# Two-layer network on one core: the S5 output products in 64-row tiles, sums of squares on TensorE, nine low parts on GpSimd

## The chip, the cores and the metric

The kernel runs on one core of one Trainium2 chip. The metric is the device time of one execution in microseconds; it is given as the median of several runs, and one further execution was profiled.

## What is computed

The reference is a chain of two small networks over 512 positions and 1024 features: a convolution and pooling mixer, a gated linear recurrence, a normalisation, then an S5 state-space mixer, a gated unit, two MLPs, and windowed attention. What matters here is the S5 mixer, and the two normalisations ahead of it:

```python
x1 = rmsnorm(h, final_norm)            # end of the first network
hn = rmsnorm_2(x1, norm_mix[0])        # both need sums of squares over the features
# S5: 64 groups of 16 features, 64 complex states each
x_t = a * x_(t-1) + B u_t              # a, B complex, per group
y_t = Re(C x_t) + d * u_t              # = c_re . x_re - c_im . x_im
y   = gelu(y) @ w_glu ...
```

## The kernel before

Features lie on the partitions and time along the free axis. Every large matrix product is computed in three passes (`mm3`, lines 308 to 310): a weight chunk is loaded (`raw`), ScalarE copies its high part (`hi`), and VectorE or GpSimd subtracts to get the low part (`lo`). `prep` sends `lo` to GpSimd (POOL) for the chunk numbers in the set `on_pool`, else to VectorE (DVE). Chunks 107 to 109 are the last three of `w_out_odd`, 110 to 113 the small projections `w_proj`, 114 and 115 the first two of `w_glu`. There are two `raw` buffers, so the load of a chunk waits for the low part of the chunk two before it.

The work is laid out by a scheduler, and where it says `with self.after()` an instruction is pinned behind the TensorE instruction recorded before it. Each engine runs its queue in order.

**The way into S5.** The last product of the recurrence, `w_out_odd`, ends each of its eight output tiles m in `odd_out`: DVE adds the residual (`h`), ScalarE (ACT) makes a time-reversed copy (`xc`), POOL issues two DMAs that bring it back as the S5 input U (`du<-xc`, then `U<-du`), and two squares per tile are made by ACT (`xr`) and added up by DVE (`acc`), plain and scaled with the norm's weight. At the start of S5, TensorE turns the two accumulators into column sums (`columns`, line 368), and a chain of small DVE operations makes the factors by which U is scaled, six of the eight tiles on POOL and two on DVE.

**The S5 loop** runs over eight feature tiles ft. `states(ft)`: 16 TensorE matmuls (line 1251) make the inputs of the states in a PSUM bank; DVE turns them by a rotation (`a`, `b`), adds, runs two scans, turns them back (`c`, `b`), and combines real and imaginary parts of each half of the partitions in four operations of 64 partitions into the tile `e` (line 1273 sets its first column to zero). `leave(ft)`: for each of 8 groups, two matmuls with the matrix M of the chunk's inner part (line 1291) and two with the output matrix O over `e` (line 1293), 128 rows each, 64 columns of weights for either half f of the output; ACT then applies gelu and the result goes out and back by DMA. `states(ft + 1)` stands ahead of `leave(ft)` on TensorE. Between them stand blocks of the small projections (six `mm3` matmuls each, `fillers`), later pieces of the `w_glu` product (`part`). A float32 matmul shows as two rows in the trace.

**The tables** for S5 are computed in the first stage, interleaved with other work. `stored` writes the output matrices to DRAM (`tO`, line 1072), four DMAs of 64 partitions for each half q.

Of the kernel before, what the change touches and what calls it, by code (L numbers as in the profile page):

```python
# [11 lines left out]
AF = mybir.ActivationFunctionType  # L12
ALU = mybir.AluOpType
# [155 lines left out]
class Kern:  # L169
# [5 lines left out]
    SQX, EPOS = (0, 2, 5), (4, 4)  # L175
    TAPP = ()
    BOOST = 400
    on_pool = frozenset(n for n in range(107) if n > 57 or n % 2 or n < 6)

    def __init__(self, ctx, tc, I, O, vat, cat):  # L180
        self.tc, self.nc, self.I, self.O = tc, tc.nc, I, O
# [226 lines left out]
    def consts(self):  # L408
        nc = self.nc
        self.vecs = self.p_const.tile([128, self.I["vecs"].shape[1]], F32, name="vecs")  # L410
        nc.sync.dma_start(out=self.vecs, in_=self.I["vecs"])
        ct = self.p_const.tile([128, self.I["consts"].shape[1]], F32, name="ctile")
        nc.scalar.dma_start(out=ct, in_=self.I["consts"])
        C = lambda n: ct[:, self.cat[n][0]:self.cat[n][0] + self.cat[n][1]]
        self.ident, self.fix, self.eye16, self.chunk, self.not0 = (C(n) for n in ("ident", "fix", "eye16", "chunk", "not0"))
        self.half, self.own = C("half"), C("own")
        self.halfpi = self.p_const.tile([128, 1], F32, name="halfpi")
        nc.gpsimd.memset(self.halfpi, 1.5707963267948966)
        self.ones = self.p_const.tile([128, 128], F32, name="ones")
# [8 lines left out]
        self.tab, self.U, self.acc12 = [], [], []  # L428
        self.ft, self.behind, self.ticks = None, [], 0


# [301 lines left out]
    def odd(self, h):  # L733
        nc = self.nc
        xg = [self.split(h[k], self.X(), self.V("g_odd", k)) for k in range(8)]
        acc = self.square_sum(h)
# [4 lines left out]
        for n in range(-self.LAG, 12):  # L741
# [23 lines left out]
            x, i, gt = (t[:, n % G] for t in grp)  # L765
# [10 lines left out]
        for ms in self.ODD_MS:  # L776
            os = {m: self.bank(("mm", "mm", "mm", "sp", "sp", "yp", "yp", "mm")[m]) for m in ms}
            for q in range(2):
                for m in ms:
                    w = self.get_w()  # L780
                    for k in range(6):
                        self.mm3(os[m], w, k, ysp[6 * q + k], q + k == 0, q == 1 and k == 5)
                    if q == 1:
                        out[m] = self.odd_out(m, os[m], h[m])
        return out

    def lru(self, x, i, gt):
# [25 lines left out]
    def odd_out(self, m, o, h):  # L813

        n = self.H("h3")
        v = lambda a: a.rearrange("p (c s) -> p s c", s=8)
        self.add(n.rearrange("p (s c) -> p s c", s=8), v(o), v(h))
        if len(self.tab):


            r = self.L("xc", 2 + self.LAG)
            self.act(r.rearrange("p (s c) -> p s c", s=8), n.rearrange("p (s c) -> p s c", s=8)[:, ::-1], AF.Copy)
            du = self.dram.tile([128, T], F32, name=f"du{m}")
            self.nc.gpsimd.dma_start(out=du.rearrange("(s h) (g c) -> h g s c", s=8, g=8).rearrange("h g s c -> (h g) s c"),
                                     in_=r.rearrange("p (s c) -> p s c", s=8))
            U = self.p_xg.tile([128, 8, 64], F32, tag="xg", name="U")
            self.nc.gpsimd.dma_start(out=U.rearrange("p g c -> p (g c)"), in_=du)
            self.U.append(U)

            for k, g in enumerate((1.0, self.V("g_fin1", m))):  # L830
                q = self.L(*(self.sq if m else ("acc", 2)))
                self.act(q, n, AF.Square, scale=g)
                if m == 0:
                    self.acc12.append(q)
                else:
                    self.add(self.acc12[k], self.acc12[k], q)
        return n


# [19 lines left out]
    def odd_vectors(self):  # L859
# [16 lines left out]
        self.ts(q, lam, -1.0, ALU.mult, 0.0, ALU.max)  # L876
        self.stt(q, p, 2.0, q, ALU.mult, ALU.add)
        C = lambda nm, w: self.p_const.tile([128, w], F32, name=nm)
        self.sp4 = C("sp4", 12)
        self.ts(self.sp4, q, 4.0, ALU.mult)  # L880

# [95 lines left out]
    def tables(self, small):  # L977
# [16 lines left out]
        for ft in range(8):  # L994
# [14 lines left out]
            for q in range(2):  # L1009
# [58 lines left out]

                def stored(q=q, orr=orr, oi=oi, tO=tO):
                    for k, w in enumerate((orr, oi)):  # L1070
                        for g2 in range(2):
                            nc.sync.dma_start(out=tO[64 * k:64 * k + 64, 512 * q:512 * q + 512].rearrange("n (a g m) -> n g a m", a=2, g=2)[:, g2],
                                              in_=w[64 * g2:64 * g2 + 64].rearrange("p a j h -> p a (j h)"))

                late(stored)
                if q == 1:
# [77 lines left out]
    def s5(self, h, fill, glu):  # L1154
# [40 lines left out]
        def behind(f, *a, **k):  # L1195
            with self.after():
                f(*a, **k)
# [3 lines left out]
                behind(*next(blocks))  # L1201

        fillers(self.FILL[0])
        st = self.bank("st")
        for k in range(2):
            behind(self.columns, self.acc12[k], st, 4 * k)
        fillers(self.FILL[1])
        s = self.p_s.tile([128, 24], F32, tag="st", name="st_s")
        v, t = s[:, 0:8], s[:, 8:12]
# [30 lines left out]
        def states(ft):  # L1240
# [20 lines left out]
            self.mul(b[:, 1], sp[:, 0], N)  # L1261
            self.add(a[:, 0], a[:, 0], b[:, 0])
            self.sub(a[:, 1], a[:, 1], b[:, 1])
            for r in range(2):
                z = a[:, r].rearrange("p a c -> p (a c)")
                nc.vector.tensor_tensor_scan(out=z, data0=dec.rearrange("p a c -> p (a c)"), data1=z, initial=0.0, op0=ALU.mult, op1=ALU.add)


            e, c = f4(), f4()
            self.tt(c, a, c2, ALU.mult)  # L1270
            self.mul(b[:, 0], a[:, 1], N, nc.gpsimd if ft in self.B0P else None)
            self.mul(b[:, 1], a[:, 0], N, nc.gpsimd if ft in self.B1P else None)
            nc.vector.memset(e[:, :, :, 0:1], 0.0)
            for r, op in ((1, ALU.add), (0, ALU.subtract)):
                for q in range(2):
                    rows = slice(64 * q, 64 * q + 64)
                    self.tt(e[64 * r:64 * r + 64, q, :, 1:64], c[rows, r, :, 0:63], b[rows, r, :, 0:63], op)
            live[ft] = O, M, u, e

        def leave(ft):  # L1280
            O, M, u, e = live.pop(ft)
# [14 lines left out]
            nc.scalar.dma_start(out=dy, in_=y.rearrange("p g c -> p (g c)"))  # L1296
# [533 lines left out]
```

## Time and profile before

| | us |
|---|---|
| median of 3 runs | 1884.67 |
| lowest, highest | 1882.24, 1885.48 |
| the profiled execution's own time | 1886.16 |
| its span, first to last instruction | 1884.3 |
| TensorE busy in it | 1764.2 (94%) |
| VectorE, ScalarE, GpSimd busy | 1167.2, 762.0, 456.6 |

The profile has one line for each group of instructions, a list of who waited for whom, and a timeline. "PE" is TensorE, "PEld" its weight loads, SPq the DMA queue that loads the weights. An idle time in square brackets names what ended it. A line can be that of a helper, so instructions are told apart by the tiles that they write and read.

### The profile page before, as it was taken

Reading aid. Unit: us, or ns where it says so; the run is one execution under the profiler, and the core shown is the slowest. Engines: PE = TensorE matmul, PEld = TensorE weight load, DVE = VectorE, ACT = ScalarE, POOL = GpSimd, SP = SyncE. Lnnn points to the kernel's source line nnn. Section 1 sums busy time; section 2 is a strip of 40 time slices with the busy share of each in tenths; the row PEclk is TensorE's granted clock in tenths of the full one; section 3 lists DMA queues with packets and bytes.
Section 4 is the critical chain, followed back from the end, with each engine's and each line's share of the span. In section 5 each row is a group of like instructions: output and inputs, shape, how many; then the busy total and the mean of one; then the engine's idle time right before and its main releaser. Section 6 shows DMA issues by size and latency. Waiting matters only on the chain.

```text
span 1884.3 us, 24650 instructions
## 1 busy us (share of the span) xinstructions
PE 1764.2 (94%) x9298; PEld 1439.7 (76%) x9298; DVE 1167.2 (62%) x1885; ACT 762.0 (40%) x1330; POOL 456.6 (24%) x422
## 2 busy tenths in 40 slices
PE   7797999999887897899999999998999999999997
PEld 5685778877765776687888888887778888888886
DVE  9989777555888859655432344578686642244456
ACT  4334444443554462234432332335665432233234
POOL 5464667333666643100000000032000000000002
PEclk8898999999988898899999999999999999999998
DMA  4598443331222488523232222333111233322322
GB/s 167 136 225 213 128 129 123 119 104 65 76 75 76 136 244 291 169 92 112 93 100 91 100 100 91 101 106 110 41 55 45 101 101 91 100 101 91 100 94 91
DMA packets 128871, 215.93 MB, mean 115 GB/s; under 512 B 40048, under 2 KB 79728, under 8 KB 128752
## 3 DMA queue, kind: packets, MB, share of 16 engines
q1 hardware_dynamic: 108144, 189.27, 32.5%
q10 hardware_dynamic: 17968, 16.43, 2.6%
q0 software_dynamic: 2640, 8.65, 1.4%
q8 instruction: 73, 1.20, 0.3%
q14 instruction: 46, 0.38, 0.1%
HBM read 187.44 MB, written 26.21 MB: 113 GB/s over the span
## 4 chain that ended last, share of the span: by engine, by line
PE 68%; DVE 14%; issue 5%; POOL 4%; ACT 4%; DMA 3%; SPq 1%; ACTq 0%; DVEq 0%; POOLq 0%
PE mm L308 19%; PE mm L310 19%; PE mm L309 19%; POOL lo L252 2%; DVE lo L252 1%; DVE e L808 1%; ACT hi L249 1%; PE pv L1609 1%; SPq L1175 1%; PE sc L309 1%; PE sc L308 1%; PE sc L310 1%; DVE pl L264 1%; DVE srm L267 1%; DVE h L264 1%
## 5 line engine op out<-in xcount | busy, mean ns | idle before, releaser
L249 ACT ACTIVATE hi<-raw 128x1024 fp32r<-128x1024 f32 (+1 forms) x280 | 292.4, 1046 | 672.8 <-PE mm L309 552.4
L252 DVE TENSOR_TENSOR lo<-raw,hi 128x1024 fp32r<-128x1024 f32 (+1 forms) x211 | 262.1, 1243 | 422.1 <-ACT hi L249 417.3
L310 PE MATMUL mm<-xg,lo 128*128 128x512 f32 x924 | 361.0, 391 | 9.4 <-DVE lo L252 8.1
L308 PE MATMUL mm<-xg,hi 128*128 128x512 f32 x924 | 363.2, 394 | 5.1 <-ACT hi L249 1.8
L309 PE MATMUL mm<-xg,hi 128*128 128x512 f32 x924 | 360.2, 390 | 0.3 <-DVE xg L252 0.2
L1423 POOL DMA_DIRECT2D pj<-proj x16 | 8.8, 549 | 1025.8 <-DVE t L264 784.0
L308 PE MATMUL mm<-hid,hi 128*128 128x512 f32 (+1 forms) x648 | 250.7, 387 | 1.8 <-DVE t L252 1.8
L309 PE MATMUL mm<-hid,hi 128*128 128x512 f32 (+1 forms) x648 | 250.3, 387 | 0.0
L310 PE MATMUL mm<-hid,lo 128*128 128x512 f32 (+1 forms) x648 | 250.1, 386 | 0.0
L310 PEld LDWEIGHTS mm<-xg,lo 128*128 128x128 f32 x924 | 173.8, 188 | 48.0 <-DVE lo L252 9.0
L308 PEld LDWEIGHTS mm<-xg,hi 128*128 128x128 f32 x924 | 173.8, 188 | 44.9 <-ACT hi L249 2.3
L252 POOL TENSOR_TENSOR lo<-raw,hi 128x1024 fp32r<-128x1024 f32 (+1 forms) x69 | 170.6, 2473 | 146.8 <-ACT hi L249 140.6
L309 PEld LDWEIGHTS mm<-xg,hi 128*128 128x128 f32 x924 | 173.8, 188 | 36.4 <-DVE xg L252 1.4
L308 PEld LDWEIGHTS mm<-hid,hi 128*128 128x128 f32 x648 | 121.7, 188 | 26.6 <-DVE t L252 2.0
L310 PEld LDWEIGHTS mm<-hid,lo 128*128 128x128 f32 x648 | 121.7, 188 | 24.6
L309 PEld LDWEIGHTS mm<-hid,hi 128*128 128x128 f32 x648 | 121.7, 188 | 24.6
L308 PE MATMUL mm<-y,hi 128*128 128x512 f32 x192 | 78.6, 409 | 10.2 <-ACT y L249 8.9
L309 PE MATMUL mm<-y,hi 128*128 128x512 f32 x192 | 76.8, 400 | 0.0
L310 PE MATMUL mm<-y,lo 128*128 128x512 f32 x192 | 76.5, 399 | 0.0
L309 PE MATMUL mm<-big,hi 128*128 128x512 f32 x160 | 64.5, 403 | 3.9 <-DVE big L264 3.9
L308 PE MATMUL mm<-big,hi 128*128 128x512 f32 x160 | 65.3, 411 | 2.2 <-ACT hi L249 2.2
L310 PE MATMUL mm<-big,lo 128*128 128x512 f32 x160 | 64.2, 402 | 0.1
(468 smaller groups left out, 3086.1 us busy)
## 6 DMA issues: line engine op xcount, KB each, us to landing
raw<-in_w_up SPq DMA_DIRECT2D x64, 512.0 KB
raw<-in_w_down SPq DMA_DIRECT2D x64, 512.0 KB
raw<-in_w_in_even SPq DMA_DIRECT2D x40, 512.0 KB
raw<-in_w_in_odd SPq DMA_DIRECT2D x24, 512.0 KB
raw<-in_w_out_even SPq DMA_DIRECT2D x16, 512.0 KB
raw<-in_w_glu SPq DMA_DIRECT2D x16, 512.0 KB
raw<-in_w_gate SPq DMA_DIRECT2D x16, 512.0 KB
raw<-in_w_out_odd SPq DMA_DIRECT2D x16, 384.0 KB
```

The costliest lines, as they stand in the source:

```text
L249: self.nc.scalar.activation(out=out, in_=in_, func=func, scale=scale, bias=bias)
L252: (eng or self.nc.vector).tensor_tensor(out=out, in0=a, in1=b, op=op)
L264: self.nc.vector.scalar_tensor_tensor(out=out, in0=a, scalar=s, in1=b, op0=op0, op1=op1)
L267: (eng or self.nc.vector).tensor_scalar(out=out, in0=a, scalar1=s1, scalar2=s2, op0=op0, **({} if op1 is None else {"op1": op1}))
L308: mm(out, hi[:, sl], xh, start=start, stop=False)
L309: mm(out, hi[:, sl], xl, start=False, stop=False)
L310: mm(out, lo[:, sl], xh, start=False, stop=stop)
L808: nc.vector.tensor_tensor_scan(out=y, data0=u[:, k], data1=x[:, k], initial=0.0, op0=ALU.mult, op1=ALU.add)
L1175: nc.sync.dma_start(out=M0[:, 128 * g:128 * g + 128], in_=bass.AP(k0.tensor, k0.offset + 4096 * g, [[16, 8], [256, 16], [1, 128]]))
L1423: self.nc.gpsimd.dma_start(out=p, in_=pj[m])
L1609: mm(o, l, r[:, w], start=n == 0, stop=n == 6 * nk - 1)
```

## The change

- DVE no longer builds the tile `e`. It makes four products (`c` for both parts in one operation, and `e` with one sign flipped) and TensorE adds them: each group now has the two matmuls with M and eight with O, over 64 rows each (`tile_position=(64*q, 64*f)`) and 63 columns of `c` or `e`. The addition before the scans becomes one operation.
- One square per tile is left in `odd_out`. TensorE sums it with two weight columns (ones and the squared norm weight, the new constant `g12`), four matmuls per tile m, after the matmuls of tile m + 1; the last after the first four blocks of the projections. The DVE additions and `columns` over the accumulators go.
- `on_pool` reaches to chunk 115: nine low parts move from DVE to POOL.
- `stored` writes `tO` in two DMAs of 128 partitions in place of four, in another layout that `enter` reads with the same loads.

```diff
-    on_pool = frozenset(n for n in range(107) if n > 57 or n % 2 or n < 6)
+    on_pool = frozenset(n for n in range(116) if n > 57 or n % 2 or n < 6)
...
                     if q == 1:
                         out[m] = self.odd_out(m, os[m], h[m])
+                        if m and self.squares:
+                            self.squares.pop(0)()
...
-            for k, g in enumerate((1.0, self.V("g_fin1", m))):
-                q = self.L(*(self.sq if m else ("acc", 2)))
-                self.act(q, n, AF.Square, scale=g)
-                if m == 0:
-                    self.acc12.append(q)
-                else:
-                    self.add(self.acc12[k], self.acc12[k], q)
+            q = self.L(*self.sq)
+            self.act(q, n, AF.Square)
...
+            def summed():
+                for b in range(4):
+                    with self.after():
+                        self.nc.tensor.matmul(st[:, b], q[:, 128 * b:128 * b + 128], self.g12[:, m], start=m + b == 0, stop=m == 7 and b == 3)
...
-                        for g2 in range(2):
-                            nc.sync.dma_start(out=tO[64 * k:64 * k + 64, 512 * q:512 * q + 512].rearrange("n (a g m) -> n g a m", a=2, g=2)[:, g2],
-                                              in_=w[64 * g2:64 * g2 + 64].rearrange("p a j h -> p a (j h)"))
+                        nc.sync.dma_start(out=tO[:, 512 * k + 256 * q:512 * k + 256 * q + 256], in_=w.rearrange("p a j h -> p (a j h)"))
...
-        for k in range(2):
-            behind(self.columns, self.acc12[k], st, 4 * k)
+        for f in self.squares:
+            f()
...
-            self.add(a[:, 0], a[:, 0], b[:, 0])
-            self.sub(a[:, 1], a[:, 1], b[:, 1])
+            self.add(a, a, b)
...
-            nc.vector.memset(e[:, :, :, 0:1], 0.0)
-            for r, op in ((1, ALU.add), (0, ALU.subtract)):
-                for q in range(2):
-                    rows = slice(64 * q, 64 * q + 64)
-                    self.tt(e[64 * r:64 * r + 64, q, :, 1:64], c[rows, r, :, 0:63], b[rows, r, :, 0:63], op)
+            self.stt(e[:, 0], a[:, 1], -1.0, N, ALU.mult, ALU.mult)
+            self.mul(e[:, 1], a[:, 0], N)
...
-                    for f, o in enumerate(os):
-                        nc.tensor.matmul(o, O[g // 4][:, g % 4, 64 * f:64 * f + 64], e[:, q, a4, :], start=False, stop=True)
+                    rows = slice(64 * q, 64 * q + 64)
+                    for r in range(2):
+                        for x in e:
+                            for f, o in enumerate(os):
+                                nc.tensor.matmul(o[:, 1:64], O[r][rows, a4, 64 * f:64 * f + 64], x[rows, r, a4, 0:63], start=False, stop=r == 1 and x is e[1], tile_position=(64 * q, 64 * f))
```

The order of the instructions on TensorE at `leave(0)`, first before, then after. `sp<-U,x` is `states`, `yp<-U,gt` the products with M, `yp<-xs,i` those with O:

```order
L310 MATMUL mm<-y,lo 128x512
L1251 MATMUL sp<-U,x 64x64 x16
L1291 MATMUL yp<-U,gt 64x64 x4
L1293 MATMUL yp<-xs,i 64x64 x2
L1291 MATMUL yp<-U,gt 64x64 x2
```

```order
L310 MATMUL mm<-y,lo 128x512
L1261 MATMUL sp<-U,x 64x64 x16
L1294 MATMUL yp<-U,gt 64x64 x2
L1300 MATMUL yp<-xs,i 64x63 x8
L1294 MATMUL yp<-U,gt 64x64 x2
```

In both the last two rows alternate until eight groups are done; between two pairs of M products there now stand eight O products where there were two.

On POOL, where S5 begins, before and then after (`U<-du` brings in an S5 input, `xc<-ctile` is a decay table, `U<-U,xc` the scaling):

```order
L824 DMA du_6335<-xc 128x8x64
L827 DMA U<-du_6297 128x512
L824 DMA du_6373<-xc 128x8x64
L827 DMA U<-du_6335 128x512
L827 DMA U<-du_6373 128x512
L824 DMA du_6436<-xc 128x8x64
L827 DMA U<-du_6436 128x512
L252 TENSOR_TENSOR xc<-ctile,m_436 128x512 x4
L252 TENSOR_TENSOR U<-U,xc 128x512 x6
```

```order
L827 DMA du_6305<-xc 128x8x64
L830 DMA U<-du_6267 128x512
L252 TENSOR_TENSOR lo<-raw,hi 128x1024
L827 DMA du_6343<-xc 128x8x64
L830 DMA U<-du_6305 128x512
L252 TENSOR_TENSOR lo<-raw,hi 128x1024
L830 DMA U<-du_6343 128x512
L252 TENSOR_TENSOR lo<-raw,hi 128x1024
L827 DMA du_6406<-xc 128x8x64
L252 TENSOR_TENSOR lo<-raw,hi 128x1024
L830 DMA U<-du_6406 128x512
L252 TENSOR_TENSOR xc<-ctile,m_436 128x512 x4
```

The four low parts of the projections, which DVE made, now stand among the DMAs that bring in U.

## Rows read from the trace of the kernel before

**Rows 1.** Stages: length, busy (count) of PE, PEld, DVE, ACT, POOL, clock, DMA.

```profile
660.00:700.00 40.00, 38.67 (x170) 31.42 (x170) 25.09 (x29) 23.12 (x36) 19.43 (x19) 1.00 0.82 249
...
729.00:790.00 61.00, 46.15 (x765) 38.59 (x764) 53.38 (x111) 14.43 (x28) 13.45 (x12) 0.84 0.71 215
```

**Rows 2.** Waits of PE, 640 to 830 us: total, times, longest.

```profile
PE yp L1293 <- DVE xs L252: 13.5, 4, 6.0
PE mm L308 <- ACT y L249: 8.9, 3, 6.8
...
PE mm L308 <- DVE h L252: 1.3, 1, 1.3
```

**Rows 3.** Timeline of PE around leave(2): start, length, line, operands, count.

```profile
738.59 0.39 PE L309 MATMUL mm<-y,hi 128*128 128x512 f32 x1
738.82 0.40 PE L310 MATMUL mm<-y,lo 128*128 128x512 f32 x1
739.14 1.15 PE L1251 MATMUL sp<-U,x 128*64 128x64 f32 x32
...
741.64 0.34 PE L1293 MATMUL yp<-xs,i 128*64 128x64 f32 x4 [1.11 <-DVE xs L252]
741.81 0.29 PE L1291 MATMUL yp<-U,e 128*64 128x64 f32 x4
...
743.21 0.29 PE L1293 MATMUL yp<-xs,i 128*64 128x64 f32 x4
743.42 0.50 PE L308 MATMUL mm<-y,hi 128*128 128x512 f32 x1
```

**Rows 4.** Timeline of PE in the attention, where matmuls of 64 rows stand.

```profile
1327.98 0.28 PE L1556 MATMUL sc<-k,q 64*128 64x256 f32 x1
1328.10 0.28 PE L1557 MATMUL sc<-k,q 64*128 64x256 f32 x1
1328.31 0.50 PE L308 MATMUL mm<-o,hi 128*128 128x512 f32 x1
1328.65 0.40 PE L309 MATMUL mm<-o,hi 128*128 128x512 f32 x1
```

**Rows 5.** Timeline of PE at two blocks of column sums.

```profile
704.88 3.41 PE L368 MATMUL st<-ones,acc 128*128 128x1 f32 x16
...
884.86 0.95 PE L368 MATMUL st<-ones,acc 128*128 128x1 f32 x8
885.67 0.49 PE L308 MATMUL mm<-xg,hi 128*128 128x512 f32 x1
```

**Rows 6.** Timeline of DVE, chain of states(0); last row, states(3).

```profile
718.74 2.94 DVE L252 TENSOR_TENSOR xs<-xs 128x256 f32<-128x256 f32 x2
721.60 3.36 DVE L1266 TENSOR_TENSOR_SCAN xs<-xc,xs 128x256 f32<-128x256 f32 x2
724.88 1.19 DVE L252 TENSOR_TENSOR lo<-raw,hi 128x1024 fp32r<-128x1024 f32 x1
...
727.38 1.74 DVE L252 TENSOR_TENSOR xs<-xs 64x252 f32<-64x252 f32 x4
...
753.44 0.75 DVE L252 TENSOR_TENSOR xs<-xs 128x256 f32<-128x256 f32 x2
```

**Rows 7.** Low parts on POOL (page, costliest groups): busy, mean ns, idle before.

```profile
L252 POOL TENSOR_TENSOR lo<-raw,hi 128x1024 fp32r<-128x1024 f32 (+1 forms) x69 | 170.6, 2473 | 146.8 <-ACT hi L249 140.6
```

**Rows 8.** Timeline of ACT and POOL at the way into S5, ACT inside the loop.

```profile
699.57 1.06 ACT L249 ACTIVATE hi<-raw 128x1024 fp32r<-128x1024 f32 x1 [2.63 <-DMA raw<-in_w_proj]
...
706.96 0.55 POOL L827 DMA_DIRECT2D U<-du  x1 [4.61 <-DMA du<-xc]
...
774.60 1.06 ACT L249 ACTIVATE hi<-raw 128x1024 fp32r<-128x1024 f32 x1 [6.25 <-DMA raw<-in_w_glu]
```

**Rows 9.** Issues of the table's stores: count, ns min/median/max, first and last start.

```profile
L1072 SPq DMA_DIRECT2D tO<-tq_wr x32: 577/587/1778, 82.1 to 366.5; - x32
```

**Rows 10.** Waits of DVE, up to 400 us: total, times, longest.

```profile
DVE tq_wr L252 <- DMA tO<-tq_wr: 5.8, 2, 5.2
```

More of the change, by code (lines that the diff above doesn't have):

```diff
@@ L427, in consts @@
         self.act(warm, self.halfpi, AF.Silu)
-        self.tab, self.U, self.acc12 = [], [], []
+        self.tab, self.U, self.squares = [], [], []
         self.ft, self.behind, self.ticks = None, [], 0
@@ L828, in odd_out @@
             self.U.append(U)
-            for k, g in enumerate((1.0, self.V("g_fin1", m))):
-                q = self.L(*(self.sq if m else ("acc", 2)))
-                self.act(q, n, AF.Square, scale=g)
-                if m == 0:
-                    self.acc12.append(q)
-                else:
-                    self.add(self.acc12[k], self.acc12[k], q)
+            q = self.L(*self.sq)
+            self.act(q, n, AF.Square)
+            if m == 0:
+                self.st12 = self.bank("st")
+            st = self.st12[:, 0:8].rearrange("p (j b) -> p b j", j=2)
+            def summed():
+                for b in range(4):
+                    with self.after():
+                        self.nc.tensor.matmul(st[:, b], q[:, 128 * b:128 * b + 128], self.g12[:, m], start=m + b == 0, stop=m == 7 and b == 3)
+            self.squares.append(summed)
         return n
@@ L878, in odd_vectors @@
         C = lambda nm, w: self.p_const.tile([128, w], F32, name=nm)
+        self.g12 = C("g12", 16).rearrange("p (k j) -> p k j", j=2)
+        nc = self.nc
+        nc.vector.memset(self.g12[:, :, 0:1], 1.0)
+        self.mul(self.g12[:, :, 1], self.V("g_fin1", 0, 8), self.V("g_fin1", 0, 8))
         self.sp4 = C("sp4", 12)
@@ L1203, in s5 @@
         fillers(self.FILL[0])
-        st = self.bank("st")
-        for k in range(2):
-            behind(self.columns, self.acc12[k], st, 4 * k)
+        for f in self.squares:
+            f()
+        st = self.st12
         fillers(self.FILL[1])
@@ L1260, in states @@
             self.mul(b[:, 0], sp[:, 1], N)
-            self.mul(b[:, 1], sp[:, 0], N)
-            self.add(a[:, 0], a[:, 0], b[:, 0])
-            self.sub(a[:, 1], a[:, 1], b[:, 1])
+            self.stt(b[:, 1], sp[:, 0], -1.0, N, ALU.mult, ALU.mult)
+            self.add(a, a, b)
             for r in range(2):
@@ L1266, in states @@
                 nc.vector.tensor_tensor_scan(out=z, data0=dec.rearrange("p a c -> p (a c)"), data1=z, initial=0.0, op0=ALU.mult, op1=ALU.add)
-            e, c = f4(), f4()
+            c, e = f4(), f4()
             self.tt(c, a, c2, ALU.mult)
-            self.mul(b[:, 0], a[:, 1], N, nc.gpsimd if ft in self.B0P else None)
-            self.mul(b[:, 1], a[:, 0], N, nc.gpsimd if ft in self.B1P else None)
-            nc.vector.memset(e[:, :, :, 0:1], 0.0)
-            for r, op in ((1, ALU.add), (0, ALU.subtract)):
-                for q in range(2):
-                    rows = slice(64 * q, 64 * q + 64)
-                    self.tt(e[64 * r:64 * r + 64, q, :, 1:64], c[rows, r, :, 0:63], b[rows, r, :, 0:63], op)
-            live[ft] = O, M, u, e
+            self.stt(e[:, 0], a[:, 1], -1.0, N, ALU.mult, ALU.mult)
+            self.mul(e[:, 1], a[:, 0], N)
+            live[ft] = O, M, u, (c, e)
         def leave(ft):
```

## The prediction

> **What bounds the kernel now.** I read the page's busy shares first: TensorE works 94% of the span, so an instruction taken from another engine is worth only what TensorE waited for it, and one added on TensorE costs its whole length wherever TensorE has no idle time. Then the stretches in which the change lies. On the way into S5 (660 to 700 us) TensorE is busy 38.67 of 40 us at full clock: nothing hides there. In the S5 loop (729 to 790 us) it is busy 46.15 of 61, VectorE 53.38, and the granted clock is 0.84 [rows 1]. The list of waits says what the idle time was: TensorE waited 13.5 us in four goes for the states (`xs`) from VectorE, the longest 6.0, and 8.9 in three for ScalarE's gelu output, nearly all of it one wait of 6.8 [rows 2]. So some 15 us of the loop is not TensorE's; the rest is. The question is whether the new products cost more than those waits.
>
> **The change part by part.** Times are made against the profiled execution, 1886.16 us, which is 1.49 over the median of 1884.67; each sum is carried to the median by taking that off.
>
> 1. *Squares on TensorE, in `w_out_odd`.* Eight blocks of eight trace rows, 128 x 1. A block of just that shape took 884.86 to 885.67, 0.81 us, until the next product began [rows 5]. One of the first seven falls where TensorE waits 1.3 for `h` anyway [rows 2]; six are paid: 6 x 0.81 = +4.9 (bounds +2.5, half the price, to +5.7, all seven). The squares and additions that go lie on ScalarE and VectorE beside a full TensorE: nothing.
>
> 2. *The column sums.* The 16 rows at 704.88 took 3.41 us [rows 5], twice what two blocks of 0.81 would make, which I put down to a lower clock. Eight remain: -1.7. Against it, the low part of chunk 110 is now POOL's: 2.47 us [rows 7] where VectorE takes 1.19 [rows 6], so +1.3; the second chunk after it gets its buffer later, and ScalarE already waited 2.63 for the load there [rows 8]. Net -0.4. POOL makes these low parts between its DMA issues, one of which waited 4.61 for its source [rows 8]; a low part queued behind such a wait would cost up to that, so the bounds are -1.7 and +2.9.
>
> 3. *The first chain of states.* Its last four operations take 1.74, and a low part of 1.19 stands in the middle of it [rows 6]; both leave VectorE, -2.9. But an operation with two SBUF inputs stretches while POOL works: the two additions took 2.94 here and 0.75 in states(3) [rows 6], 2.2 more. POOL's scalings are there in both kernels, and one low part of 2.47 follows them now. I take -2.0, nearer the gain since most of what stretched the chain was there already; bounds -2.9 and +1.4 (two such stretches against the gain).
>
> 4. *The products.* This is the large term. A `leave` had 64 trace rows on TensorE; it now has 160, two for each instruction. From 741.81 to 743.21 TensorE got through 48 rows, 0.029 us each [rows 3]. The rows of weights don't show in this price: products of 64 rows by 256 columns start 0.12 apart [rows 4], and 0.12 for four times the columns is the same speed. So 96 x 0.029 = 2.8 us for a leave. To it comes the change of form: M is multiplied in tiles of 128 rows, O in tiles of 64, and they alternate, 15 changes inside a leave. What does one cost? Where the column width changes, 738.82 to 739.14 is 0.32 instead of 0.23, and 743.21 to 743.42 is 0.21 instead of 0.12: 0.09 each [rows 3]; a first pair after such a place took 0.17 (741.64 to 741.81) instead of 0.12, another 0.05. From tiles of 64 rows by 128 to whole ones it is 0.21 against 0.12 at 1328.10, and 0.34 against 0.23 for the next [rows 4], 0.20 together. No row shows a change of the rows alone at 64 columns, so from nothing to 0.20; I take 0.14, the sum from the rows of the same loop. 15 x 0.14 = 2.1. A leave grows by 4.9, eight by +39.2. Bounds +22.4 (changes free) to +46.4 (0.20 each).
> The Trainium skill ("TensorEngine Tiling (Array Packing)", section Key Properties) says that changing the tiling mode, not just the tile, drains TensorE; rows 3 and 4 show such a gap at every change that they hold. By it the sum keeps its 2.1 a leave; without it the sum would be 16.8 lower.
>
> 5. *Waits for the states.* A leave is now about 6.8 us (160 x 0.029 + 2.1), and each chain on VectorE is 1.74 shorter less a little for larger operations. VectorE had 53.38 us of work for the loop [rows 1]; with eight chains shorter and a loop longer by more than 20 us it no longer holds TensorE. Only the first wait, 6.0, has no leave ahead of it. 13.5 - 6.0 = -7.5 (bounds 0 and -10.5, half of the first gone as well).
>
> 6. *The wait for gelu's output, 6.8* [rows 2]. ScalarE's copies stand behind the high part of a `w_glu` chunk that waited 6.25 for its load [rows 8], and that load waited for a buffer, which a low part on VectorE set free. VectorE is less loaded and the leave ahead is 4.9 longer, but the leave's own end moves too. I take 2.8 of it (bounds 0 and -6.8).
>
> 7. *The clock.* A mean of 0.84 over 61 us [rows 1] is 19.5 us at the lower level, 1.2 GHz, and 9.8 us of work lost. Before it fell TensorE had waited. Of 22.4 us of waits [rows 2] 10.3 go by steps 5 and 6, but the longest for the states stays: less than that share, -2.0 (bounds 0 and -4.5).
>
> 8. *The table's stores.* 32 of 64 issues remain; the 32 that go are 0.577 each [rows 9], 18.5 us of SyncE's queue over 284 us. On VectorE 5.8 us of waiting hung on these stores, nearly all in one wait [rows 10], and part of that VectorE work is on the path of a TensorE that has idle time in the first stage. I take -2.0, a third; bounds -5.8 and +2.5 (the shift of table work to other places, of the size of one low part).
>
> Five `w_glu` products that move from the last leave to behind it are only traded in order, and TensorE is full there: nothing.
>
> Sum: 4.9 - 0.4 - 2.0 + 39.2 - 7.5 - 2.8 - 2.0 - 2.0 = +27.4. That is 1913.6 in the profiled execution, 1912.1 for the median.
>
> **The rivals.**
>
> *The change of row tiles costs nothing* (column width stays at 64, and only width changes stand in rows 3). Then step 4 is 22.4, the sum +10.6, the median about 1895. Against it is the gap in rows 4, which holds both changes at once.
>
> *Faster: the small tiles run beside each other.* The four 64 x 64 tiles of the array would work at once, or two of them, so that eight O products pass nearly in the time of the two before, whose four rows took 0.12 [rows 3]. Then a leave grows by only a third of 2.8, some 0.9, for starts and ends, and the waits still shorten: 39.2 becomes 7.4, the sum -4.4, the median about 1880; without step 1's price, 1875. It decides between faster and slower when a leave grows by under 1.5 us, (39.2 - 27.4)/8. For it: only the pace of whole-height tiles is shown by the rows of the loop. Against: products of one group stay in one half of the rows, add into the same output, and two column tiles alternated in the old code at 0.029 already.
> The Trainium skill (same page and section) says that different tiles can load weights and multiply in parallel. No row of before shows it.
>
> *Slower: the clock stays at its lower level.* Many small products in place of large ones may be granted less. If the loop, now about 88 us long, ran at 1.2 GHz for half of it in place of 19.5 us, some 24 us at the lower level more, TensorE would do 12 us less work in it, the median 1924; at that level throughout, over 1940. For it: 0.84 already [rows 1]. Against: the falls stand behind waits that go.
>
> *Gains and losses cancel:* changes free, and steps 3, 5, 6, 7 and 8 at their better ends: 4.9 - 1.7 - 2.9 + 22.4 - 10.5 - 6.8 - 4.5 - 5.8 = -4.9 is the extreme, so no change is within reach.
>
> **How the numbers follow.** The forecast, slower by 27, has 0.62; free changes 0.15; small tiles beside each other 0.09; the low clock 0.07; cancelling 0.07. The likeliest case alone runs from 1899 to 1922: about -13 and +10, step 4's bounds with part of the others'. The range should hold the time 8 times in 10: it takes in free changes and most of cancelling's upper half, so it begins at 1886, and it ends at 1926 with the milder half of the low clock. A measurement of this kernel can tell about 0.2%, 3.8 us, from no change. Faster 0.09; same 0.07; slower 0.62 + 0.15 + 0.07 = 0.84.
>
> **What would show it.** A leave from its first to its last `yp` row about 6.8 us; a gap of some 0.2 where M's and O's products meet; the waits for `xs` down to the first; blocks of squares 0.8 apart from the next product; POOL's low parts among the DMAs of U; the loop about 88 us in place of 61, at a clock of 0.84 or better. The prediction is wrong if eight O products take less than 0.3 us, or if the loop's clock is much below 0.8.

## The result, and the profile after

The changed kernel takes 1915.92 us, median of 4 runs (1914.43 to 1917.02), beside 1883.45 for the kernel before, median of 4 runs. The ratio is 1.0167, 95% interval [1.0154, 1.0181]: slower by 32.5 us. Forecast were 1912 and slower by 27. The two profiled executions are nearer to each other than the medians, 1886.16 and 1914.43, 28.3 apart, because that of before was above its median and that of after the fastest of its four. The places below are read from these two.

The page of the changed kernel, first line of its busy times: TensorE has 43.4 us more work, VectorE 30 less, GpSimd 21 more.

```profile
PE 1807.6 (95%) x10114; PEld 1475.6 (77%) x10114; DVE 1137.4 (59%) x1816; ACT 758.2 (40%) x1322; POOL 477.5 (25%) x431
```

Where did 28 us come from? Both kernels do the same 6720 products of `mm3` on TensorE, in the same order but for five of `w_glu` at the last leave, so the start of one and the same product in both timelines can be subtracted. That gives a ledger, in us:

| place (time in before) | after minus before | step between |
|---|---|---|
| 649.6, tables and recurrence are done | +0.3 | tables: +0.3 |
| 695.2, near the end of `w_out_odd` | +8.1 | squares: +7.8 |
| 710.9, behind the column sums | +0.3 | -7.8 |
| 714.0, behind the product of the scaling factors | +5.0 | +4.7 |
| 731.9, behind the first leave | +12.1 | +7.0 |
| 793.6, behind the loop | +27.6 | +15.6 |
| 1846.5 | +28.0 | +0.4 |

Behind 794 us the difference stays between 27.4 and 28.4. Before 650 us it goes up and down, between -1.9 and +4.3, and ends at +0.3. The whole change is decided in 145 us.

The loop first. TensorE's timeline in leave(1), columns as in [rows 3]:

```profile
746.83 1.98 PE L1261 MATMUL sp<-U,x 128*64 128x64 f32 x32
748.59 0.36 PE L1294 MATMUL yp<-U,gt 128*64 128x64 f32 x4
748.88 0.68 PE L1300 MATMUL yp<-xs,O 64*64 64x63 f32 x16
749.49 0.34 PE L1294 MATMUL yp<-U,gt 128*64 128x64 f32 x4
749.76 0.68 PE L1300 MATMUL yp<-xs,O 64*64 64x63 f32 x16
750.37 0.34 PE L1294 MATMUL yp<-U,gt 128*64 128x64 f32 x4
...
755.01 0.68 PE L1300 MATMUL yp<-xs,O 64*64 64x63 f32 x16
755.62 0.50 PE L308 MATMUL mm<-y,hi 128*128 128x512 f32 x1
```

From 748.59 to 755.62, 7.03 us, where 64 rows at the 0.029 of [rows 3] made 1.9 and the forecast was 6.8. A group goes from 749.49 to 750.37, 0.875 us for 4 rows of M and 16 of O. At 0.029 a row that is 0.58; 0.295 are left for two changes of form, 0.147 each. Forecast: 0.14.

The waits of TensorE from 640 to 860 us, where [rows 2] stood before (total, times, longest):

```profile
PE st L1207 <- DVE xc L252: 5.7, 1, 5.7
PE yp L1300 <- DVE xs L264: 2.1, 1, 2.1
PE yp L1300 <- DVE xs L252: 2.1, 1, 2.1
```

Of 13.5 us of waits for the states 4.2 are left, all in the first leave; the 6.8 for gelu's output is gone altogether. (`xs` by L264 and by L252 are two operations of VectorE in the same chain.) A new wait stands there, 5.7 us for the factors by which U is scaled.

Last, the clock. These are stretches of five us, columns as in [rows 1], first of before and then of after:

```profile
700.00:705.00 5.00, 3.23 (x13) 2.29 (x11) 2.43 (x3) 3.87 (x8) 1.00 (x2) 0.86 0.66 197
705.00:710.00 5.00, 5.00 (x21) 4.62 (x20) 2.79 (x5) 1.52 (x2) 3.02 (x4) 0.50 1.00 361
710.00:715.00 5.00, 5.00 (x29) 3.53 (x28) 2.77 (x14) 1.42 (x3) 1.30 (x2) 0.61 1.01 371
```

```profile
700.00:705.00 5.00, 5.00 (x27) 4.27 (x26) 1.13 (x1) 2.21 (x4) 3.82 (x3) 1.00 0.69 233
705.00:710.00 5.00, 5.00 (x27) 4.27 (x26) 0.14 (x1) 2.87 (x6) 1.92 (x2) 1.00 0.72 222
710.00:715.00 5.00, 2.71 (x12) 1.88 (x10) 4.76 (x8) 1.64 (x3) 4.45 (x4) 1.00 1.00 366
```

Before, TensorE was idle twice around 700 us:

```profile
699.38 0.50 PE L308 MATMUL mm<-y,hi 128*128 128x512 f32 x1 [1.33 <-DVE h L252]
702.81 0.50 PE L308 MATMUL mm<-y,hi 128*128 128x512 f32 x1 [1.77 <-ACT y L249]
```

Then it ran at the lower level, 1.2 GHz, for some ten us; the column sums fell into that. After, it has no idle time there and keeps the full clock. That is the -7.8 of the ledger: the two waits that are gone make 3.4 of it, the column sums 2.7, and the clock of the products around them 1.7. It then stands at the factors, 710 to 720 busy for 4.3 of 10 us, and 4.7 of the 7.8 are gone again.

That the idle time made the clock fall is not shown. In all nine traces with the squares on TensorE the granted clock is 1.00 from 700 to 710, and in four of the five without it falls between 700 and 715; but in the fifth, the kernel with the products alone (below), TensorE waited there too, 1.28 and 1.46 us, and kept the full clock:

```profile
700.00:705.00 5.00, 2.25 (x9) 1.29 (x8) 3.97 (x5) 3.49 (x6) 1.47 (x2) 1.00 0.79 239
705.00:710.00 5.00, 5.00 (x31) 4.37 (x31) 1.50 (x4) 2.70 (x5) 0.90 (x2) 1.00 0.89 295
```

### The profile page after: what moved, and what is told of

Its sections match the earlier page's. It is cut to its first block, busy times and chain, and to the rows that moved or that the text cites. A ratio compares the mean times of both kernels' runs of the same rounds, so it can differ in the third digit from the quotient of the medians.

```text
span 1912.6 us, 26158 instructions
## 1 busy us (share of the span) xinstructions
PE 1807.6 (95%) x10114; PEld 1475.6 (77%) x10114; DVE 1137.4 (59%) x1816; ACT 758.2 (40%) x1322; POOL 477.5 (25%) x431
## 4 chain that ended last, share of the span: by engine, by line
PE 71%; DVE 14%; issue 4%; POOL 4%; ACT 3%; DMA 2%; SPq 1%; ACTq 0%; DVEq 0%; POOLq 0%
PE mm L308 20%; PE mm L310 19%; PE mm L309 19%; PE yp L1300 2%; POOL lo L252 2%; PE pv L1616 1%; DVE lo L252 1%; DVE e L811 1%; PE yp L1294 1%; ACT hi L249 1%; PE sc L309 1%; PE sc L308 1%; PE sc L310 1%; SPq L1185 1%; DVE srr L252 1%
## 5 line engine op out<-in xcount | busy, mean ns | idle before, releaser
L252 DVE TENSOR_TENSOR lo<-raw,hi 128x1024 fp32r<-128x1024 f32 x202 | 251.0, 1243 | 413.4 <-ACT hi L249 407.6
L252 POOL TENSOR_TENSOR lo<-raw,hi 128x1024 fp32r<-128x1024 f32 (+1 forms) x78 | 189.3, 2429 | 145.7 <-ACT hi L249 136.6
```

The costliest lines, as they stand in the source:

```text
L252: (eng or self.nc.vector).tensor_tensor(out=out, in0=a, in1=b, op=op)
```

## Experiments

### One change each

The O products alone, on the kernel before. VectorE's part and the layout of the table come with them; the table is still stored by four DMAs a half.

```diff
-            for r, op in ((1, ALU.add), (0, ALU.subtract)):
-                for q in range(2):
...
-                    self.tt(e[64 * r:64 * r + 64, q, :, 1:64], c[rows, r, :, 0:63], b[rows, r, :, 0:63], op)
...
+            self.stt(e[:, 0], a[:, 1], -1.0, N, ALU.mult, ALU.mult)
+            self.mul(e[:, 1], a[:, 0], N)
...
-                    for f, o in enumerate(os):
-                        nc.tensor.matmul(o, O[g // 4][:, g % 4, 64 * f:64 * f + 64], e[:, q, a4, :], start=False, stop=True)
...
+                    for r in range(2):
+                        for x in e:
+                            for f, o in enumerate(os):
+                                nc.tensor.matmul(o[:, 1:64], O[r][rows, a4, 64 * f:64 * f + 64], x[rows, r, a4, 0:63], start=False, stop=r == 1 and x is e[1], tile_position=(64 * q, 64 * f))
```

> The kernel before, with the four products on VectorE, the O products in tiles of 64 rows and the table stored in the layout that they read, still by four DMAs a half. Theory (a leave grows by 4.9 to 5.1 us, eight by 40, of which 12 to 15 come back out of waits for VectorE and ScalarE and from the clock): 24 to 30 us slower than before, so nearly the whole change. Rival (the products cost at most half of the change and the entry into S5, POOL and the squares make the rest): under 18 us slower.

1902.70 us, median of 4 runs (1901.38 to 1906.72), ratio to before 1.0093 [1.0074, 1.0112]: 17.5 slower, on the rival's side of 18 by a hair. Its profiled execution is the slowest of the four, and there the ledger reads +21.3 behind the loop. So the products are between half and three quarters of the change, less than the theory had said. Its waits show why it isn't 40:

```profile
PE st L1196 <- DVE xc L252: 4.0, 1, 4.0
PE yp L1289 <- DVE xs L252: 3.1, 1, 3.1
...
PE mm L308 <- ACT y L249: 1.5, 1, 1.5
```

Of 13.5 us of waits for the states [rows 2] 3.1 are left. The 1.5 for ScalarE's output stands at 704.8, on the way into S5, as 1.77 of the 8.9 did at 702.81 in the kernel before; in the loop that wait went from 7.1 to nothing. So 17.5 of the 41 us by which eight leaves grow were idle time that they fill. The wait for the factors is there without squares and without POOL's low parts, in an execution in which TensorE kept its full clock ahead of it; in the other three kernels that keep the old squares it is 0.7 to 2.5.

The squares alone:

```diff
-            for k, g in enumerate((1.0, self.V("g_fin1", m))):
-                q = self.L(*(self.sq if m else ("acc", 2)))
-                self.act(q, n, AF.Square, scale=g)
...
+            q = self.L(*self.sq)
+            self.act(q, n, AF.Square)
...
+                        self.nc.tensor.matmul(st[:, b], q[:, 128 * b:128 * b + 128], self.g12[:, m], start=m + b == 0, stop=m == 7 and b == 3)
```

> The kernel before, with the squares summed by TensorE, nothing else. Theory (a block of 0.8 to 0.95 us in a full TensorE, eight times, less the 1.7 us of half of the column sums): 3 to 6 us slower than before. Rival (ScalarE's and VectorE's eight squares and fourteen additions held something, and the blocks fall into waits): 1 us slower to 3 us faster.

1889.02 us, median of 10 runs, ratio 1.0017 [1.0006, 1.0027]: 3.8 slower, as the theory had it, but not by its sum. Its ledger rises by 9.3 from 650 us to the end of `w_out_odd`, gives 7.8 of it back up to the end of the column sums, again by the two waits and the clock, and then meets a wait for the factors of 3.7:

```profile
PE yp L1305 <- DVE xs L252: 12.2, 5, 4.1
PE mm L308 <- ACT y L249: 7.2, 3, 6.8
PE st L1209 <- DVE xc L252: 3.7, 1, 3.7
```

The waits of the loop are those of before. They go with the products, not with the squares.

POOL's nine low parts put back, in the changed kernel:

```diff
-    on_pool = frozenset(n for n in range(116) if n > 57 or n % 2 or n < 6)
+    on_pool = frozenset(n for n in range(107) if n > 57 or n % 2 or n < 6)
```

> The changed kernel, with the low parts of chunks 107 to 115 back on VectorE. Theory (POOL's low part of the last projection chunk ahead of the decay tables moves those tables into VectorE's chain of small operations, which then stretch, two of them to 3.67 us in place of 0.37): TensorE's wait of 5.7 for the scaling factors falls under 2.5, 3 to 5 us faster than the changed kernel, 1911 to 1913. Rival (a low part of 1.2 us in the same chain on VectorE and others in the states' chains take that back): 1915 to 1918.

1911.20 us, median of 4 runs, ratio 1.0135 [1.0115, 1.0154], 26.0 over before in place of 32.5: inside the theory's range, and the ledger is 3.9 lower behind the loop, 23.7 in place of 27.6. But it is not gained where the theory put it. VectorE's operations from the column sums to the factors take 6.4 us in place of 8.4, and the wait for the factors fell from 5.7 to 3.7, not under 2.5; yet in this execution TensorE came there 2.0 later, and the product of the factors starts at 718.36 in place of 718.45. The gain, 3.4, comes up to the end of the first leave. VectorE's last operations of the first chain, in the changed kernel and then with the low parts on VectorE (start, length, operation):

```profile
730.30 2.56 DVE L264 SCALAR_TENSOR_TENSOR xs<-xs,y 128x256 f32<-128x256 f32 x1
732.78 0.41 DVE L252 TENSOR_TENSOR xs<-xs,y 128x256 f32<-128x256 f32 x1
```

```profile
731.58 0.41 DVE L264 SCALAR_TENSOR_TENSOR xs<-xs,y 128x256 f32<-128x256 f32 x1
731.91 0.41 DVE L252 TENSOR_TENSOR xs<-xs,y 128x256 f32<-128x256 f32 x1
```

In the changed kernel POOL makes the low part of chunk 114 from 729.79 on, 2.78 us, and the operation that meets it takes 2.56 in place of 0.41. TensorE stops a second time in its first leave for that (2.1 above). Then it runs at 1.2 GHz to about 749, in the other kernel to about 744:

```profile
735.00:740.00 5.00, 5.00 (x71) 4.06 (x67) 2.82 (x6) 0.38 (x1) 0.00 (x0) 0.50 0.02 3
740.00:745.00 5.00, 5.00 (x61) 4.22 (x60) 0.00 (x0) 0.38 (x1) 0.00 (x0) 0.50 0.03 10
745.00:750.00 5.00, 5.00 (x69) 3.95 (x69) 1.15 (x3) 0.00 (x0) 0.00 (x0) 0.62 0.41 121
```

```profile
735.00:740.00 5.00, 5.00 (x76) 4.18 (x76) 1.99 (x5) 0.39 (x1) 0.00 (x0) 0.50 0.08 30
740.00:745.00 5.00, 5.00 (x58) 3.78 (x54) 0.04 (x1) 0.98 (x2) 0.00 (x0) 0.58 0.44 133
745.00:750.00 5.00, 5.00 (x120) 4.26 (x119) 4.83 (x7) 0.39 (x1) 2.58 (x2) 1.00 1.02 315
```

That the second stop makes the low clock last longer fits these rows, but it is not shown to be what costs: the kernel with four stores a half (below), which has the same instructions here, stopped once in its first leave, 3.29 us, ran at 1.2 GHz to about 748, and its ledger behind that leave is 11.8 where the changed kernel has 12.1. There the low part stretched another operation of the chain, to 2.65 us.

To see which low part lengthens the wait for the factors, the one right ahead of POOL's decay tables (chunk 113) alone went back:

```diff
-    on_pool = frozenset(n for n in range(116) if n > 57 or n % 2 or n < 6)
+    on_pool = frozenset(n for n in range(116) if n != 113 and (n > 57 or n % 2 or n < 6))
```

> The changed kernel with one low part, that of the last projection chunk (113), on VectorE. Theory (it is this one, on POOL right ahead of the decay tables, that pushes the tables into VectorE's chain of small operations): TensorE's wait of 5.7 for the factors becomes 3.7 or less, the run 2 to 4 us faster, 1912 to 1914. Rival (the low part on VectorE stands in the same chain, 1.2 us, and the wait stays within 1 us of 5.7; then POOL's other low parts hold the tables back): 1915 to 1917.

1913.88 us, median of 4 runs, ratio 1.0149 [1.0134, 1.0163]. The time is in the theory's range and too near to 1915.92 to tell; the wait is 4.8, within 1 us of 5.7, so the theory falls. So does the rival's reason, that POOL's other low parts hold the tables back. VectorE and POOL there:

```profile
714.63 0.17 DVE L252 TENSOR_TENSOR rs_s<-rs_s,st_s 128x8 f32<-128x8 f32 x1
714.83 3.55 DVE L264 SCALAR_TENSOR_TENSOR rs_s<-rs_s 128x8 f32<-128x8 f32 x2
```

```profile
714.54 0.55 POOL L830 DMA_DIRECT2D U<-du  x1 [5.13 <-DMA du<-xc]
715.11 3.04 POOL L252 TENSOR_TENSOR xc<-ctile,m 128x512 f32<-128x512 f32 x3
```

POOL had no low part to make. It stood 5.13 us at the issue of the last `U<-du`, which waits for the DMA ahead of it, and the three tables behind that issue start only then, in the middle of VectorE's chain, where two operations on 128 x 8 take 3.55 in place of 0.37. In the kernel before this issue waited too, 4.61 [rows 8], but TensorE was late by its low clock, and the tables met only the start of the chain, where one operation took 1.68 us.

The stores put back to four a half:

```diff
-                        nc.sync.dma_start(out=tO[:, 512 * k + 256 * q:512 * k + 256 * q + 256], in_=w.rearrange("p a j h -> p (a j h)"))
+                        for g2 in range(2):
+                            nc.sync.dma_start(out=tO[64 * g2:64 * g2 + 64, 512 * k + 256 * q:512 * k + 256 * q + 256], in_=w[64 * g2:64 * g2 + 64].rearrange("p a j h -> p (a j h)"))
```

> The changed kernel, with the table stored by four DMAs of 64 partitions for each half, in the new layout. Theory (the 32 issues that went were beside other work; up to 640 us the two traces differ by less than 1 us): within 3 us of the changed kernel, 1913 to 1919. Rival (the products, the squares and POOL's low parts alone came to 28 of the 32 us, and the stores are the other 4.7): 1909 to 1912.

1913.56 us, median of 4 runs (1910.62 to 1917.60), ratio 1.0153 [1.0134, 1.0171]: as the theory had it, no difference that these runs can tell. It is 28.6 over its own before, where the changed kernel had 32.5, with intervals that overlap; the ledgers behind the loop, 27.2 and 27.6, show no 4.7 that fewer stores cost.

### What a change of tile costs, and what runs side by side

All eight M products of a half first, then its O products:

```diff
-                        nc.tensor.matmul(o, M[:, 128 * g + 64 * f:128 * g + 64 * f + 64], u[:, g, :], start=True, stop=False)
...
+                        nc.tensor.matmul(o, M[:, 128 * g + 64 * f:128 * g + 64 * f + 64], u[:, g, :], start=a4 == 0, stop=False)
+                for a4 in range(4):
...
+                            for f, o in enumerate(os[a4]):
```

> The changed kernel, with the eight M products of a half first and its thirty-two O products behind them, so that a leave changes between tiles of 128 and of 64 rows 4 times (3 more than before) in place of 16. Theory (the changes cost): a leave of the changed kernel takes 0.875 us a group for 20 rows, 0.58 at 0.029 a row, which leaves 0.147 for each change; 12 changes fewer in eight leaves, 12 x 0.147 x 8 = -14 us against the changed kernel, about 1902, more if leaves at the lower clock are shortened too. Rival (the products of 64 rows are slower by themselves, 0.038 us a row, and the changes are free): a leave keeps its 7.0 us, 1916 within 2 us.

1905.70 us, median of 4 runs, ratio 1.0103 [1.0085, 1.0122]: 20.5 over before where the changed kernel had 32.5, 12 us less for 12 changes fewer in each leave; the theory had 14. A leave:

```profile
752.97 1.15 PE L1261 MATMUL sp<-U,x 128*64 128x64 f32 x32
753.95 0.64 PE L1295 MATMUL yp<-U,e 128*64 128x64 f32 x16
754.52 2.09 PE L1300 MATMUL yp<-xs,i 64*64 64x63 f32 x64
756.53 0.69 PE L1295 MATMUL yp<-U,e 128*64 128x64 f32 x16
757.15 2.08 PE L1300 MATMUL yp<-xs,i 64*64 64x63 f32 x64
759.16 0.50 PE L308 MATMUL mm<-y,hi 128*128 128x512 f32 x1
```

5.21 us in place of 7.03: 1.82 for 12 changes, 0.152 each. Sixty-four O rows with the change behind them take 2.01, so a row is 0.029 as before. The rival, slow small products and free changes, falls. In the profiled execution the ledger behind the loop is only 5.8 lower than that of the changed kernel: TensorE waits 1.32 for the states in the last leave, and the granted clock is 0.56 and then 0.50 from 800 to 810.

M first for both halves, and O alternating between the upper and the lower 64 rows:

```diff
...
+            for a4 in range(4):
+                for r in range(2):
+                    for x in e:
+                        for f in range(2):
+                            for q in range(2):
+                                rows = slice(64 * q, 64 * q + 64)
+                                nc.tensor.matmul(yp[q][64 * f:64 * f + 64, a4, 1:64], O[r][rows, a4, 64 * f:64 * f + 64], x[rows, r, a4, 0:63], start=False, stop=a4 == 3 and r == 1 and x is e[-1], tile_position=(64 * q, 64 * f))
```

> The changed kernel, with all sixteen M products of a leave first and then the O products, alternating between the upper and the lower 64 rows, which add into two different banks. Theory (tiles of 64 rows pass one after the other at 0.029 us a row of the trace, whichever half they are in): a leave of 160 x 0.029 + 2 changes of 0.14 = 5.0 us, as with the M products grouped by halves, 1902 to 1907. Rival (tiles in different halves of the rows run side by side): the 128 O rows take 1.9 in place of 3.7, a leave 3.2, 15 us less in eight, 1888 to 1893.

1889.72 us, median of 10 runs, ratio 1.0022 [1.0011, 1.0033]: the rival. The same instructions as in the grouped kernel, in another order, are 16 us faster; two changes fewer in a leave are 2.4 of it.

```profile
746.13 1.10 PE L1295 MATMUL yp<-U,e 128*64 128x64 f32 x32
747.16 2.09 PE L1302 MATMUL yp<-xs,i 64*64 64x63 f32 x128
749.18 0.50 PE L308 MATMUL mm<-y,hi 128*128 128x512 f32 x1
```

128 rows of O pass in 2.02 us with the change behind them, the time that 64 had: 0.0146 a row. Tiles in the two halves of the rows do run side by side, when neighbours in the queue lie in different halves. In the changed kernel the sixteen rows of a group lie in one half. The halves add into two different banks here, so the bank changes with the half, and no run changes one without the other; that it is not the bank alone is argued from the 32 M rows of this leave, which change the bank at every second product and take 1.03 us with the change behind them, 0.028 a row. The Trainium skill, "TensorEngine Tiling (Array Packing)", section Key Properties, says that different tiles load and multiply in parallel; these rows agree for the two row halves, and the pace of 0.029 in one half shows that two column tiles in turn gain nothing over what they had in the full height.

### Fewer products

VectorE adds its two pairs of products, and TensorE has four O products a group:

```diff
-            live[ft] = O, M, u, (c, e)
+            self.add(c, c, e)
+            live[ft] = O, M, u, (c,)
```

In the changed kernel, with M grouped by halves:

> The changed kernel with M products grouped by halves, and VectorE adding its two pairs of products in one operation, so that TensorE has four O products a group in place of eight. Theory (TensorE is the bound in the loop, and each row costs 0.029): 64 rows fewer in a leave, 8 x 64 x 0.029 = -15 against the grouped one (1906), so 1889 to 1893. Rival (VectorE's addition of 0.7 to 1.2 us in each chain, with a leave of 3.3 us ahead of it, brings the waits for the states back): over 1897.

1893.53 us, median of 4 runs, ratio 1.0044 [1.0029, 1.0059], 12 less than grouped alone where 15 were expected, just above the theory's range; the waits for the states are 9.0 again in three goes. In the kernel before, with its old squares and low parts, and M grouped by halves:

> The kernel before (its squares, its column sums, its low parts) with the four products on VectorE, added there in one operation, and four O products a group, M products grouped by halves. Theory (a leave of 96 rows at 0.029 and four changes of 0.14, 3.3 us where it was 1.9, +11 in eight; back come the waits for the states but the first, 7.5, and part of the 6.8 for gelu): 1882 to 1890. Rival (the waits stay, since the chain on VectorE is only 1 us shorter): 1891 to 1898.

1886.65 us, median of 10 runs, ratio 1.0006 [0.9995, 1.0017]: no difference from before, in the theory's range. With row halves alternating in place of groups, first with all eight O products, then with the addition and four:

> The kernel before (its squares, column sums and low parts), with the four products on VectorE and the O products, after all M products of a leave, alternating between the upper and the lower 64 rows. Theory (row halves run side by side, 128 O rows in 1.9 us, so a leave of 3.2 against 1.9, +10; waits for VectorE and ScalarE give back 12 to 15; from the changed kernel with such pairs, +5 us, less the squares' 4 and the low parts' 5 to 6): 1877 to 1883. Rival (the pairs need both halves' banks and the first half's gelu comes later, so the waits for gelu and for the banks grow by what the products give): 1884 to 1890.

1885.63 us, median of 12 runs from 1880.87 to 1890.30, ratio 1.0007 [0.9996, 1.0018]: the rival, as far as a spread of 9 us lets one say. The profiled execution is the fastest of the twelve. Its M products need both banks at once, and TensorE waits for the gelu that empties them:

```profile
PE yp L1284 <- ACT xr L249: 5.6, 1, 5.6
PE yp L1291 <- DVE xs L252: 4.7, 3, 3.2
```

> The same, with VectorE adding its two pairs of products first, so half the O products. Theory (a leave of 2.3 us, 0.9 less than with all eight, but an addition of 0.7 to 1.2 us on VectorE, which is then the later one): as the kernel with pairs and without the addition, or up to 4 us slower, 1879 to 1886. Rival (TensorE is the bound): 5 to 7 us faster than the one without, under 1877.

1878.65 us, median of 8 runs (1877.99 to 1881.76), ratio 0.9972 [0.9963, 0.9982]: 6 us faster than before, and so faster than both kernels. A leave is 2.3 us, 0.4 longer than the old one, for a chain on VectorE that has one operation of full height where four of half height stood:

```profile
758.25 1.10 PE L1285 MATMUL yp<-U,gt 128*64 128x64 f32 x32
759.28 1.16 PE L1292 MATMUL yp<-xs,O 64*64 64x63 f32 x64
760.57 0.50 PE L308 MATMUL mm<-y,hi 128*128 128x512 f32 x1
```

It had been expected at 1879 to 1886, not faster than the one without the addition; it is 7.0 faster than that one, near the rival's 5 to 7. TensorE still waits for the states 6.4 us and 10.5 for ScalarE's output, 2.5 of that on the way into S5, so the loop is not TensorE's alone. The 5.6 us at the banks are not there; that this makes the difference fits, but is not shown.

Last, the changed kernel with row halves alternating and POOL's low parts put back:

> The changed kernel with pairs of row halves and with the low parts of chunks 107 to 115 on VectorE. Theory (POOL's low parts cost 5 to 6.5 us in the way into S5 and the first states, whatever the leaves take): 1883 to 1886, against 1889.7 with POOL's. Rival (with shorter leaves VectorE is the bound, and the low parts that come back there cost what they gave): 1888 to 1892.

1889.07 us, median of 10 runs, ratio 1.0023 [1.0012, 1.0034], the same as with them on POOL, 1889.72: the rival's time. What the low parts cost on POOL they cost on VectorE once the leaves are short; where in the loop they cost it was not looked for.

## Why the prediction held, and where it was off

The direction, the size and the mechanism were right: 27.4 forecast for the profiled execution, 28.3 seen there, 32.5 between the medians. Step by step:

1. *Squares*: +4.9 forecast, +7.8 seen. Seven blocks stand ahead of the column sums, and all seven were paid. Five cost 0.95 each, the length that [rows 5] give for one, not the 0.81 to the next start: the product behind a block starts its follower some 0.1 late. The first two cost 1.9 and 1.2, with a wait of 0.7 for ScalarE's square. The wait of 1.3 for `h` went, but behind the blocks, and the ledger has it in the next step. Mis-sized, past the upper bound of 5.7.
2. *Column sums*: -0.4 forecast, -7.8 seen, and +4.7 right behind it. This step failed, in both of its halves. The low clock of the 3.41 us [rows 5] was rightly seen, but I priced only the sums at it and not the products around them, and did not ask whether the change would take away the idle time ahead, 1.33 and 1.77. And the gain was not kept, since TensorE arrived at the factors before VectorE had them. Net of steps 1 and 2: +4.5 forecast, +4.7 seen. The agreement of the sum is luck.
3. *First chain*: -2.0 forecast. From its first operation to its last the chain took 11.7 us before, 10.3 in the changed kernel and 8.5 with the low parts back on VectorE: -1.4 seen, inside the bounds. The four operations went, but the low part of chunk 114 on POOL stretched one to 2.56. Ahead of the chain, among the small operations for the factors, 2.00 beside the low part of chunk 113 and 3.67 beside the decay tables stand where the kernel before had 1.68 and 0.37. Steps 2 and 3 had asked what a low part on POOL costs by its own length; what it costs is how long VectorE's operations take beside it. With the low parts back on VectorE the whole is 6.5 faster by the medians.
4. *Products*: right in both prices. 0.029 a row; a change 0.147 to 0.152 against 0.14; a leave 7.03 against 6.8, eight +41 against +39.2. The grouped kernel shows the change's price alone. The Trainium skill's sentence that a change of mode drains TensorE (same page and section as above) agrees with this price also where only the rows change, which no row of before had shown.
5. *Waits for the states*: -7.5 forecast, 13.5 to 4.2 seen, -9.3, inside the bounds.
6. *Wait for gelu*: -2.8 forecast, -7.1 seen: the long wait and one of 0.4 went. With leaves of 7 us ahead, ScalarE's output was in time at every one. The prediction put all of the 8.9 [rows 2] into the loop; 1.77 of it stood at 702.81, on the way into S5, and its going is counted in step 2.
7. *Clock*: -2.0 forecast, next to nothing seen. From the factors to the end of the loop the mean granted clock is 0.87 over 79.9 us before and 0.90 over 102.6 after, some 20 us at the lower level in both. There is one long stretch at 1.2 GHz, in and behind the first leave, about 732 to 749, and then none in the loop. It is dear in place, since it holds nearly a whole leave: 13.5 us from 730.43 to 743.97, 2.15 of them the second stop, for what takes 7.
8. *Stores*: -2.0 forecast, +0.3 seen; nothing. The 5.8 us of VectorE's waits [rows 10] were not on the path.

From 714 us on the forecast had -2.0 + 39.2 - 7.5 - 2.8 - 2.0 = +24.9, the ledger has +22.6. The leaves and the two kinds of waits as measured, 41 - 9.3 - 7.1, make +24.6; the 2 us between are not assigned. Of the rivals, free changes are refuted by the grouped kernel. Small tiles side by side are real, but not in this order of instructions: the counterargument that a group stays in one half of the rows was the one that decided. The low clock through the loop did not come.

Open stays why the parts don't add up by medians: products 17.5, squares 3.8 and low parts 6.5 are 27.8 of 32.5, and the stores give nothing. By the profiled executions they do nearly, 21.3, 3.5 and 3.9 against 27.6 behind the loop; the products' kernel had the slowest of its four runs profiled. The first two parts were measured on the kernel before and the third on the changed kernel, so they need not add up.

## What to carry to other kernels

Work moved to a full TensorE costs rows times their pace, and each change of tile form on top; count the changes, because regrouping the same instructions gave 12 us here. Small tiles pay when neighbours in the queue lie in different row halves (here in different banks as well), and 16 us of 33 hung on that order. An engine that is off the path can still stretch VectorE's small operations, so what is moved to it should not stand beside a chain that the bound engine waits for; here that was worth 6.5 us with the long leaves and nothing with the short ones.

## What the runs showed of the hardware

- Tiles of 64 rows in different halves of the array, adding into different banks, run side by side: 0.0146 us a trace row when the halves alternate, 0.029 in one half.
- A change between tiles of 128 and of 64 rows at the same 64 columns costs about 0.15 us at the full clock.
- VectorE operations on 128 x 8, 0.17 us alone, can last as long as the GpSimd operations beside them: two took 3.67 in place of 0.37 while three tables were made, 3.04 us, on POOL, and in the kernel with four stores a half one took 3.46 beside the same three. These are the rows of the changed kernel, VectorE and then POOL:

```profile
712.91 0.17 DVE L252 TENSOR_TENSOR rs_s<-rs_s,st_s 128x8 f32<-128x8 f32 x1
713.11 3.67 DVE L264 SCALAR_TENSOR_TENSOR rs_s<-rs_s 128x8 f32<-128x8 f32 x2
...
717.02 0.37 DVE L264 SCALAR_TENSOR_TENSOR rs_s<-rs_s 128x8 f32<-128x8 f32 x2
```

```profile
713.50 3.04 POOL L252 TENSOR_TENSOR xc<-ctile,m 128x512 f32<-128x512 f32 x3
```
